# Seven products over all 16 K tiles for the second block's pairs, and a recurrence that keeps two heads' states

## The chip, the cores and the metric

One core of one Trainium2 chip runs the kernel. The metric is the time of one execution on the device, in microseconds (us), as the median of several runs; lower is better. TensorE multiplies matrices, VectorE (DVE in the profile) and ScalarE (ACT) do elementwise work, GpSimd (POOL) does a little of it and issues some transfers, SyncE (SP) issues the other transfers. PEld is TensorE's loading of weights. Rows of the profile are in us unless they say ns.

## The reference

Two transformer-like blocks follow each other on one sequence of 512 tokens of width 2048, in float32. The change touches the second block alone, and there its first projection:

```python
xn = rmsnorm_2(h, norm_gain[l])                        # 512 x 2048
proj = jnp.einsum('bsd,de->bse', xn, w_in[l])          # 2048 -> 6 * 1024
q, k, v, g_sb, x_lru, g_lru = jnp.split(proj, ...)     # 1024 columns each
...
xc = causal_depthwise_conv(x_lru, conv_w[l], conv_b[l])    # 4 taps along the tokens
r = sigmoid(xc_block @ w_a + b_a); i = sigmoid(xc_block @ w_x + b_x)   # 8 blocks of 128
a = exp(-8 * r * softplus(-lam))
u = sqrt(1 - a * a) * (i * xc)
h_t = a_t * h_(t-1) + u_t                              # along the 512 tokens
y_lru = h * silu(g_lru)
y_sb = stick_breaking_attention(q, k, v) * silu(g_sb)
out = h + concat(y_sb, y_lru) @ w_out[l]
```

x_lru is called XL in the kernel, g_lru GL and g_sb GS. Each has 1024 columns, which are eight blocks ("heads") of 128.

## The kernel before

**Products.** A float32 product is made of three matmuls: each operand is split into a high half (ScalarE casts it to float32r) and a low half (VectorE subtracts the high half from the source), and high times high, high times low and low times high are added in PSUM. `split` (L456 the cast, L457 the subtraction) does this for weights and activations. A projection has 16 K tiles of 128 rows.

**Seven products.** Columns are projected in pairs of 128-column blocks by Winograd's form of Strassen's scheme: tokens in two halves, K in two halves, the pair's two blocks as the two column halves. Seven products on sums of pieces replace eight. Each half of K has KS = 6 tiles, so 12 of the 16 K tiles go through the scheme; the last NCL = 4 are done plainly by `rest`, with two weight pieces of their own ("6" and "8"). The second block has twelve such pairs, in the order XL0, GL0, XL2, GL2, XL4, GL4, XL6, GL6, GS0, GS2, GS4, GS6 (a name with the number of its first block; texts below call the last four GS0 to GS3). `seven` emits a pair's matmuls: products 1, 4, 5, remainder, 3, remainder, 2, 7, two remainders, 9. A matmul here has 256 moving columns (half the tokens).

**Weights of a pair.** Four raw pieces (0 to 3, `load_raw`, L654, from SP) are loaded for a pair. The sums that the scheme wants are made in place, one after the other, in the raw buffers: piece 0 is read for product 1, then piece 1 is added by a transfer that adds at its destination (`sum_up`, L663, issued by GpSimd), then it is read for product 2, then VectorE adds piece 2 (L661), it is read for product 3, then a second adding transfer brings piece 3 and it is read for product 9. `produce(p, i)` splits a sum into one of four weight buffers a to d: product 1 in a, 2 in b, 4 in c, 5 in d, 3 in c once product 4 has left it, 7 in c after product 3, 9 in b after product 2. The next pair's pieces are loaded into raw buffers as they come free.

**Order.** TensorE's order is the order in which the program emits matmuls. All other engines' and queues' orders are planned over the whole program by `Plan`: each instruction gets a due time from the matmul that needs it, and at every free moment of an engine the ready instruction with the earliest due time is taken; the order found is then fixed. ScalarE, VectorE, GpSimd and SP run in that fixed order.

**Around the pairs.** `side_x2` makes the differences of the activations' quarters that the scheme needs (S1 to S4) while the v projection still runs, from copies in DRAM (x2d); the last of them is split into `big` when v is done. Results of a pair leave PSUM by `evac_a1` (L1800), `evac_b` (L1806, L1807) and `evac_a2` (L1811). XL results go into two buffers xls and to `side_lru(b)`, one call for each of the eight heads: convolution on VectorE (L1396, L1398), two products on TensorE (pss), activations on ScalarE (L1414 to L1419), the input's products on VectorE (L1420, L1421), a square root (L1429), a product on GpSimd (L1431), the scan on VectorE (L1432), the product with the gate (L1437). A head's states A, V and U take 512 columns each of the tile `ar`. There is room for four heads at a time, so the square roots, scans and gates are emitted after heads 3 and 7, for four heads. GL results are gated and stored, and fetched again by `side_lru`. Temporary tiles `e` rotate among six buffers: a new one takes the buffer of the sixth before it.

Of the kernel before, what the change touches and what calls it, by code (L numbers as in the profile page):

```python
# [16 lines left out]
P = 128  # L17
# [25 lines left out]
KS = 6  # L43
# [345 lines left out]
def hybrid_two_block_kernel(ctx: ExitStack, tc: tile.TileContext, wp, wq, wc, xT, xtok, par, lvec, cst, rg, pg, lruw, out):  # L389
# [184 lines left out]
    YO = 2 * KS * NTOK  # L574
    operands2 = Later(lambda: next_turn([("y23", [P, YO], F32R), ("ymisc", [P, KT * NTOK - YO], F32)]))
# [71 lines left out]
    def load_raw(p, r, slot):  # L647
        if p is None:
            return
        n = WS if r < 4 else NCL * P  # L650
        raw = raw_all[:, WS * slot : WS * slot + n]
        raw_slot[(p, r)] = slot
        pair_raw[(p, r)] = raw
        nc.sync.dma_start(raw, wq[p, r] if r < 4 else wc[p, r - 4])  # L654

    def sum_up(p, r, q):
# [6 lines left out]
        pool.dma_start(pair_raw[(p, r)], wq[p, q], accum_op=ALU.add)  # L663

    def produce(p, i):
# [4 lines left out]
        r = lambda k: pair_raw[(p, k)]  # L670
# [5 lines left out]
        n = NCL * P if i in (6, 8) else WS  # L676
        slot = at[place]
        w = halves(wsp_all[:, 2 * WS * slot : 2 * WS * slot + 2 * n])
# [8 lines left out]
        elif i == 4:  # L687
            load_raw(p, 4, raw_slot[(p, 1)])
        elif i == 5:
            load_raw(p, 5, raw_slot[(p, 3)])  # L690
        elif i == 6:
            w_slots[:] = [at["a"], at["d"], at["c"], at["b"]]
            load_raw(following(p), 0, raw_slot[(p, 4)])
        elif i == 8:
            load_raw(following(p), 1, raw_slot[(p, 5)])
            if p < NEW:
                sum_up(following(p), 1, 2)
        elif i == 7:
            load_raw(following(p), 2, raw_slot[(p, 2)])
            if p >= NEW:  # L700
                sum_up(following(p), 1, 2)
        elif i == 9:
            load_raw(following(p), 3, raw_slot[(p, 0)])
# [36 lines left out]
    def seven(p, ops, r, c0a, c0b, evac_a1, evac_b, evac_a2, after=None):  # L740


        HL, x23, x1s, p1s, us, wv, ts = ops
        L = 2 * HL
        X1, X2 = slice(0, HL), slice(HL, L)
        q = following(p)

        def product(i, bank, x, c, first, last, n=KS):
            w = pair_w[(p, i)]
            for j in range(n):  # L750
                for pi, (ws, xs) in enumerate(PASSES):
                    mm(r[bank][:, c], w[:, ws, j * P : (j + 1) * P], x(xs, j), first and j == 0 and pi == 0,
                       last and j == n - 1 and pi == 2)
                yield

        def rest(i, bank, c0, x1, first, last):

            w = pair_w[(p, i)]
# [10 lines left out]
        produce(p, 6)  # L769
# [3 lines left out]
        produce(p, 8)  # L773
# [1250 lines left out]
```

## Time and profile before

| | us |
|---|---|
| Median of the runs | 1689.38 (1687.52 to 1690.68) |
| The profiled execution's own time | 1691.34 |
| Its span, first to last instruction | 1689.3 |
| The twelve pairs of the second block | 1009.6 to 1279.7 of the span |

An engine's busy time is the time in which the profile shows it at work. A row of the timeline gives the start, the duration of the merged run, engine, source line, operation and tiles, the count, and in square brackets the idle time before it with what ended that. Matmuls are pipelined and the ends are modelled: the distance between starts is what they cost. The tile names of the pair stage: `wsp` weights split, `wraw` raw weights, `pj` PSUM, `y` and `x1s` the differences, `ymisc` the partial sums and the buffers xls.

### The profile page before, as it was taken

Reading aid. Unit: us, or ns where it says so; the run is one execution under the profiler, and the core shown is the slowest. Engines: PE = TensorE matmul, PEld = TensorE weight load, DVE = VectorE, ACT = ScalarE, POOL = GpSimd, SP = SyncE. Lnnn points to the kernel's source line nnn. Section 1 sums busy time; section 2 is a strip of 40 time slices with the busy share of each in tenths; the row PEclk is TensorE's granted clock in tenths of the full one; section 3 lists DMA queues with packets and bytes.
Section 4 is the critical chain, followed back from the end, with each engine's and each line's share of the span. In section 5 each row is a group of like instructions: output and inputs, shape, how many; then the busy total and the mean of one; then the engine's idle time right before and its main releaser. Section 6 shows DMA issues by size and latency. Waiting matters only on the chain.

```text
span 1689.3 us, 28307 instructions
## 1 busy us (share of the span) xinstructions
PE 1661.5 (98%) x10840; PEld 1510.2 (89%) x10840; DVE 1204.3 (71%) x2076; ACT 945.1 (56%) x1584; POOL 184.7 (11%) x205
## 2 busy tenths in 40 slices
PE   8999999999999999999999999999999999999998
PEld 8789999999999999988887779999998888888887
DVE  5784797766798989883577857998874476885433
ACT  6454566654677777673455544657643366665311
POOL 0111121111222222100000000111100000100000
PEclk9999999999999999999999999999999999999999
DMA  8435866767666566643677976666668223434233
GB/s 314 169 126 141 205 148 166 170 156 172 138 151 144 138 147 142 172 141 133 200 245 258 298 217 149 155 185 151 176 165 265 87 76 102 128 102 129 75 103 122
DMA packets 110360, 273.01 MB, mean 162 GB/s; under 512 B 11776, under 2 KB 25728, under 8 KB 108544
## 3 DMA queue, kind: packets, MB, share of 16 engines
q1 hardware_dynamic: 93712, 225.05, 41.3%
q0 software_dynamic: 16512, 46.15, 15.9%
q8 instruction: 85, 1.39, 0.3%
q14 instruction: 51, 0.42, 0.1%
HBM read 241.79 MB, written 29.36 MB: 161 GB/s over the span
## 4 chain that ended last, share of the span: by engine, by line
PE 67%; DVE 3%; DMA 2%; ACT 1%; issue 1%; SPq 0%; DVEq 0%; ACTq 0%
PE pj L489 59%; PE pmt L489 3%; PE pss L489 2%; PE ptt L492 1%; DVE wsp L457 1%; PE bank L489 1%; DMA wraw<-in_wp 1%; PE pmt L492 1%; DMA wraw<-in_wq 1%; ACT wsp L456 0%; PE pss L492 0%; DMA e<-yd 0%; DVE big L457 0%; DMA wraw<-in_wc 0%; ACT L1429 0%
## 5 line engine op out<-in xcount | busy, mean ns | idle before, releaser
L489 PE MATMUL pj<-wsp,big 128*128 128x512 f32 x3072 | 737.1, 397 | 6.5 <-DVE wsp L457 3.6
L489 PEld LDWEIGHTS pj<-wsp,big 128*128 128x128 f32 x3072 | 570.7, 188 | 138.0 <-DVE wsp L457 6.3
L457 DVE TENSOR_TENSOR wsp<-wraw,wsp 128x768 fp32r<-128x768 f32 (+3 forms) x462 | 464.8, 1012 | 232.6 <-ACT wsp L456 224.6
L456 ACT CAST wsp<-wraw 128x768 fp32r<-128x768 f32 (+3 forms) x462 | 401.2, 873 | 375.9 <-PE pj L489 283.8
L489 PE MATMUL pj<-big,wsp 128*128 128x264 f32 (+2 forms) x4224 | 541.2, 284 | 10.8 <-ACT wsp L456 7.1
L489 PEld LDWEIGHTS pj<-big,wsp 128*128 128x128 f32 x4224 | 520.6, 189 | 13.9 <-ACT wsp L456 7.5
L663 POOL DMA_DIRECT2D wraw<-in_wq x104 | 91.3, 888 | 650.4 <-DVE wsp L457 509.1
L489 PE MATMUL pj<-x,wsp 128*128 128x264 f32 x720 | 100.9, 287 | 1.9 <-DVE wsp L457 1.4
L489 PEld LDWEIGHTS pj<-x,wsp 128*128 128x128 f32 x720 | 92.5, 188 | 3.4 <-DVE wsp L457 2.3
L489 PE MATMUL pj<-x1s,wsp 128*128 128x264 f32 (+1 forms) x576 | 79.9, 289 | 3.3 <-DVE e L1800 3.3
L456 ACT CAST pt<-ptt 128x512 fp32r<-128x512 f32 (+2 forms) x96 | 50.7, 528 | 55.5 <-PE ptt L492 55.2
L457 DVE TENSOR_TENSOR pt<-ptt,pt 128x512 fp32r<-128x512 f32 (+2 forms) x96 | 59.5, 620 | 26.2 <-ACT pt L456 25.6
L489 PEld LDWEIGHTS pj<-x1s,wsp 128*128 128x128 f32 x576 | 74.6, 193 | 3.7 <-DVE e L1800 3.5
L489 PE MATMUL pss<-kk,qq 128*128 128x264 f32 x448 | 71.8, 288 | 0.0
L489 PE MATMUL pmt<-pt,vv 128*128 128x256 f32 (+1 forms) x528 | 69.3, 279 | 0.0
L489 PEld LDWEIGHTS pmt<-pt,vv 128*128 128x128 f32 x528 | 67.2, 188 | 1.6
L1271 ACT ACTIVATE e<-e,sm 128x528 f32<-128x528 f32 x64 | 47.1, 735 | 31.5 <-DVE sm L1268 31.3
L489 PEld LDWEIGHTS pss<-kk,qq 128*128 128x128 f32 x448 | 61.5, 189 | 1.3
L489 PE MATMUL pj<-y,wsp 128*128 128x256 f32 x432 | 55.6, 282 | 0.0
L489 PEld LDWEIGHTS pj<-y,wsp 128*128 128x128 f32 x432 | 53.4, 189 | 0.0
L492 PE MATMUL ptt<-ident,e 128*128 128x128 f32 x336 | 52.5, 273 | 0.0
L1268 DVE CUSTOM_DVE_ANT_0 e<-pss,ar 128x528 f32<-128x528 f32 x64 | 44.9, 702 | 7.8 <-PE pss L489 7.5
(285 smaller groups left out, 1542.0 us busy)
## 6 DMA issues: line engine op xcount, KB each, us to landing
wraw<-in_wp SPq DMA_DIRECT2D x166, 512.0 KB, 4.1
wraw<-in_wq SPq DMA_DIRECT2D x128, 384.0 KB, 3.9
wraw<-in_wq POOLq DMA_DIRECT2D x104, 384.0 KB, 5.1
wraw<-in_wc SPq DMA_DIRECT2D x64, 256.0 KB, 2.9
gated<-e SPq DMA_DIRECT2D x40, 256.0 KB, 3.1
e<-in_xT SPq DMA_DIRECT2D x28, 264.0 KB, 4.9
early<-in_xtok SPq DMA_DIRECT2D x4, 1024.0 KB, 7.4
e<-yd SPq DMA_DIRECT2D x16, 256.0 KB, 4.2
```

Of the source, the lines that this page charges most:

```text
L456: act.copy(hi, src)
L457: dve.tensor_tensor(lo, src, f(hi), ALU.subtract)
L489: _queue(nc.tensor.matmul(out, lhsT, rhs, start=start, stop=stop).ins, cost)
L492: _queue(nc.tensor.transpose(out, in_, identity).ins, 110.0)
L663: pool.dma_start(pair_raw[(p, r)], wq[p, q], accum_op=ALU.add)
L1268: dve.tensor_tensor_reduce(out=halves(x), in0=s[:, :, :HL], in1=halves(bias[:, b0 : b0 + L]), scale=1.0, scalar=3e38, op0=ALU.add, op1=ALU ...
L1271: act.activation(x, x, AF.Exp, scale=-1.0, bias=nm, accum_out=l[:, m : m + 1])
```

## The change

Pairs of the second block take KS2 = 8 tiles in each half of K, so that all 16 K tiles go through the seven products. Remainders, their pieces and their buffers are gone there. Raw pieces and weight buffers of these pairs are 1024 columns wide (before 768, and 512 for the remainders); the fourth raw buffer lies in `ar`, the fourth weight buffer takes the place of the tile `kk`. The operands of the scheme grow to eight tiles each: y23 fills its tile, x1s gets a second part in the tile `pt`, and partial sums and xls move into `ar`. The next pair's first two pieces are loaded after `produce` 4 and 5. Half of the second output block is written at once from product 2's sum (`take_t`), which saves one addition. A, V and U have room for two heads, so square roots, scans and gates are emitted after each second head. The first block's pairs are as before.

```diff
-KS = 6
+KS, KS2 = 6, 8
...
-    operands2 = Later(lambda: next_turn([("y23", [P, YO], F32R), ("ymisc", [P, KT * NTOK - YO], F32)]))
+    operands2 = Later(lambda: next_turn([("y23", [P, 2 * KS2 * NTOK], F32R)])[0])
...
     def load_raw(p, r, slot):
...
+        if p >= NEW:
+            raw = raw_all[:, 1024 * slot : 1024 * slot + 1024] if slot < 3 else ar[:, 3072:4096]
+            nc.sync.dma_start(raw, wq2[p - NEW, r])
+        else:
+            raw = raw_all[:, WS * slot : WS * slot + (WS if r < 4 else NCL * P)]
+            nc.sync.dma_start(raw, wq[p, r] if r < 4 else wc[p, r - 4])
...
     def sum_up(p, r, q):
...
-        pool.dma_start(pair_raw[(p, r)], wq[p, q], accum_op=ALU.add)
+        pool.dma_start(pair_raw[(p, r)], wq2[p - NEW, q] if p >= NEW else wq[p, q], accum_op=ALU.add)
...
     def produce(p, i):
...
-        n = NCL * P if i in (6, 8) else WS
+        n = KS2 * P if p >= NEW else NCL * P if i in (6, 8) else WS
...
+        if p < NEW:
+            w = halves(wsp_all[:, 2 * WS * slot : 2 * WS * slot + 2 * n])
+        else:
+            w = halves(wsp_all[:, 2048 * slot : 2048 * slot + 2048]) if slot < 3 else wsp3[:]
...
         elif i == 4:
-            load_raw(p, 4, raw_slot[(p, 1)])
+            if p < NEW:
+                load_raw(p, 4, raw_slot[(p, 1)])
+            else:
+                load_raw(q, 0, raw_slot[(p, 1)])
         elif i == 5:
-            load_raw(p, 5, raw_slot[(p, 3)])
+            if p < NEW:
+                load_raw(p, 5, raw_slot[(p, 3)])
+            else:
+                w_slots[:] = [at["a"], at["d"], at["c"], at["b"]]
+                load_raw(q, 1, raw_slot[(p, 3)])
...
-    def seven(p, ops, r, c0a, c0b, evac_a1, evac_b, evac_a2, after=None):
+    def seven(p, ops, r, c0a, c0b, evac_a1, evac_b, evac_a2, after=None, take_t=None):
...
+        whole = 2 * KS == KT
...
         def rest(i, bank, c0, x1, first, last):
+            if whole:
+                return
...
-        produce(p, 6)
+        if not whole:
+            produce(p, 6)
...
-        dve.tensor_tensor(ts[:], r[0][:, :HL], us[:], ALU.add)
+        if whole:
+            yield from take_t(r[0][:, :HL], us[:])
+        else:
+            dve.tensor_tensor(ts[:], r[0][:, :HL], us[:], ALU.add)
...
+    x1sb = [Later(lambda: T([P, 2, KS, H2], "x1s", F32R)), Later(lambda: T([P, 2, KS2 - KS, H2], "pt", F32R))]
+    wsp3 = Later(lambda: T([P, 2, 1024], "kk", F32R))
+    misc2 = [ar[:, 4096 + i * H2 : 4096 + (i + 1) * H2] for i in range(4)]
+    xls = [ar[:, 5120 + i * NTOK : 5120 + (i + 1) * NTOK] for i in range(2)]
...
     def side_x2():
...
-        for j in range(KS):
+        for j in range(KS2):
...
-        split(big[:, 0, :KS, H2:NTOK], big[:, 1, :KS, H2:NTOK], s4)
+        split(big[:, 0, :KS2, H2:NTOK], big[:, 1, :KS2, H2:NTOK], s4)
...
-                n = min(8, 2 * KS - 8 * k8)
-                pool.dma_start(x2d[k8, t][:, : n * P], flat(xg[:, :n]))
+                pool.dma_start(x2d[k8, t], flat(xg))
...
     def A(b):
-        return ar[:, (b % 4) * 512 : (b % 4 + 1) * 512]
+        return ar[:, (b % 2) * 512 : (b % 2 + 1) * 512]
...
     def side_lru(b):
...
-                   *([("ydone", b - 4)] if b > 3 else []))
+                   *([("ydone", b - 2)] if b > 1 else []))
...
-        if b % 4 == 3:
+        if b % 2:
...
-                for i in range(b - 3, b + 1):
+                for i in range(b - 1, b + 1):
...
-            for i in range(b - 3, b + 1):
+            for i in range(b - 1, b + 1):
                 yield when(("gl", i))
                 y = et(NTOK)
...
-                    w_slots[:] = [3, 2, 0, 1]
+                    w_slots[:] = [2, 1, 3, 0]
...
-                for k in range(0, KS, 2):
+                for k in range(0, KS2, 2):
```

## Rows read from the trace of the kernel before

**Rows 1.** The page's first part: the span, then busy time, share of the span and instructions of TensorE and VectorE.

```profile
span 1689.3 us, 28307 instructions
...
PE 1661.5 (98%) x10840; PEld 1510.2 (89%) x10840; DVE 1204.3 (71%) x2076; ACT 945.1 (56%) x1584; POOL 184.7 (11%) x205
```

**Rows 2.** The page's chain that ended last, shares of the span by line.

```profile
PE pj L489 59%; PE pmt L489 3%; PE pss L489 2%; PE ptt L492 1%; DVE wsp L457 1%; PE bank L489 1%; DMA wraw<-in_wp 1%; PE pmt L492 1%; DMA wraw<-in_wq 1%; ACT wsp L456 0%; PE pss L492 0%; DMA e<-yd 0%; DVE big L457 0%; DMA wraw<-in_wc 0%; ACT L1429 0%
```

**Rows 3.** Busy time by stretch (start:end, length, busy time and instructions of each engine, mean granted clock of TensorE, busy share of the transfer engines, GB/s): XL and GL pairs, GS0, the last three pairs; and, from a second such table, two pairs in the middle.

```profile
1009.60:1189.60 180.00, 175.78 (x1437) 172.96 (x1436) 155.62 (x241) 108.76 (x155) 24.08 (x24) 1.00 0.64 162
1189.60:1217.90 28.30, 24.98 (x183) 24.51 (x182) 23.51 (x37) 20.62 (x28) 4.61 (x4) 0.88 0.69 189
1217.90:1279.70 61.80, 61.80 (x525) 61.70 (x523) 44.48 (x70) 26.91 (x39) 4.34 (x5) 1.00 0.64 173
...
1062.08:1106.06 43.98, 43.98 (x362) 43.43 (x360) 40.40 (x64) 30.28 (x43) 6.60 (x7) 1.00 0.60 154
```

**Rows 4.** Timeline of TensorE, from 1017 to 1250.

```profile
1017.40 0.50 PE L489 MATMUL pj<-big,wsp 128*128 128x256 f32 x2 [1.15 <-ACT wsp L456]
...
1119.78 4.25 PE L489 MATMUL pj<-big,wsp 128*128 128x256 f32 x34 [0.89 <-DVE wsp L457]
...
1128.04 3.55 PE L489 MATMUL pj<-big,wsp 128*128 128x256 f32 x28 [1.62 <-DVE wsp L457]
...
1151.65 1.56 PE L489 MATMUL pss<-qq,vv 128*128 128x512 f32 x6
1153.05 1.93 PE L489 MATMUL pj<-big,wsp 128*128 128x256 f32 x15
...
1177.56 1.57 PE L489 MATMUL pj<-big,wsp 128*128 128x256 f32 x12
...
1205.83 4.21 PE L489 MATMUL pj<-x1s,wsp 128*128 128x256 f32 x18 [3.32 <-DVE e L1800]
...
1229.22 2.32 PE L489 MATMUL pj<-x1s,wsp 128*128 128x256 f32 x18
...
1248.40 1.57 PE L489 MATMUL pj<-big,wsp 128*128 128x256 f32 x12
1249.81 2.32 PE L489 MATMUL pj<-x1s,wsp 128*128 128x256 f32 x18
```

**Rows 5.** VectorE's groups by line and form, 960 to 1005, while v is projected: line, engine, operation, tiles, shapes, count, busy us, mean ns of one, idle before.

```profile
L457 DVE TENSOR_TENSOR wsp<-wraw,wsp 128x1024 fp32r<-128x1024 f32 x16 | 19.4, 1220 | 12.5 <-ACT wsp L456 12.5
```

**Rows 6.** The same view of VectorE, 1062.08 to 1106.06.

```profile
L457 DVE TENSOR_TENSOR wsp<-wraw,wsp 128x768 fp32r<-128x768 f32 x14 | 13.3, 949 | 1.9 <-ACT wsp L456 1.8
L661 DVE TENSOR_TENSOR wraw<-wraw 128x768 f32<-128x768 f32 x4 | 3.8, 951 | 0.2 <-DMA wraw<-in_wq 0.2
L457 DVE TENSOR_TENSOR wsp<-wraw,wsp 128x512 fp32r<-128x512 f32 x4 | 3.6, 890 | 0.5 <-ACT wsp L456 0.5
```

**Rows 7.** The same view of ScalarE, 960 to 1005.

```profile
L456 ACT CAST wsp<-wraw 128x1024 fp32r<-128x1024 f32 x15 | 15.7, 1048 | 11.4 <-DMA wraw<-in_wp 7.4 <-PE pj L489 3.8
```

**Rows 8.** Timeline of ScalarE: in GS0, and the cast of product 7's weights in the third GS pair.

```profile
1198.45 1.28 ACT L1429 ACT_TABLE_LOAD   x1
...
1200.40 1.28 ACT L1417 ACT_TABLE_LOAD   x1
...
1202.41 0.80 ACT L1418 ACTIVATE ar<-e,lrup 128x512 f32<-128x512 f32 x1
...
1203.64 1.55 ACT L456 CAST wsp<-wraw 128x768 fp32r<-128x768 f32 x2
...
1248.48 0.84 ACT L456 CAST wsp<-wraw 128x768 fp32r<-128x768 f32 x1 [3.59 <-PE pj L489]
```

**Rows 9.** Timeline of VectorE: the split into big before the pairs; the low half of product 7's weights in GL6; GS0; the low halves for product 3 and 7 in the third GS pair.

```profile
997.48 1.76 DVE L457 TENSOR_TENSOR big<-ar,big 128x1536 fp32r<-128x1536 f32 x1 [0.44 <-ACT big L456]
...
1179.61 0.96 DVE L457 TENSOR_TENSOR wsp<-wraw,wsp 128x768 fp32r<-128x768 f32 x1
...
1203.77 0.69 DVE L1421 SCALAR_TENSOR_TENSOR ar<-e,ar 128x512 f32<-128x512 f32 x1 [0.44 <-ACT e L1419]
...
1205.36 0.42 DVE L1800 TENSOR_TENSOR e<-pj,ymisc 128x256 f32<-128x256 f32 x1
...
1243.75 0.96 DVE L457 TENSOR_TENSOR wsp<-wraw,wsp 128x768 fp32r<-128x768 f32 x1 [0.21 <-ACT wsp L456]
...
1249.40 0.95 DVE L457 TENSOR_TENSOR wsp<-wraw,wsp 128x768 fp32r<-128x768 f32 x1
```

**Rows 10.** The adding transfers of line L663, 1018 to 1280 (23 of them): time from GpSimd's issue to landing.

```profile
DMA to landing us min/median/max: 4.7/5.3/7.0
```

**Rows 11.** The transfers of 1217.9 to 1259 (41.1 us): the queue of GpSimd's transfers with packets, MB and share of the 16 engines' time, and SP's loads of raw pieces with count, size and median time to landing.

```profile
q0 software_dynamic: 576, 1.57, 25.6%
...
wraw<-in_wq SPq DMA_DIRECT2D x8, 384.0 KB, 4.1
```

**Rows 12.** Timeline of GpSimd: the adding transfer after the split for product 3 in the third GS pair.

```profile
1245.11 0.87 POOL L663 DMA_DIRECT2D wraw<-in_wq  x1 [12.69 <-DVE wsp L457]
```

**Rows 13.** Line L1429 (the square roots) over the whole span: count, duration in ns (least, median, most), first and last start.

```profile
L1429 ACT ACT_TABLE_LOAD  x8: 1283/1283/1283, 1061.4 to 1205.8; - x8
L1429 ACT ACTIVATE ar<-ar x8: 631/632/634, 1062.7 to 1207.1; 128x512 f32<-128x512 f32 x8
```

More of the change, by code (lines that the diff above doesn't have):

```diff
@@ L388, in hybrid_two_block_kernel @@
 @with_exitstack
-def hybrid_two_block_kernel(ctx: ExitStack, tc: tile.TileContext, wp, wq, wc, xT, xtok, par, lvec, cst, rg, pg, lruw, out):
+def hybrid_two_block_kernel(ctx: ExitStack, tc: tile.TileContext, wp, wq, wq2, wc, xT, xtok, par, lvec, cst, rg, pg, lruw, out):
     nc = tc.nc
@@ L738, in fm_all, with product @@
         return fm(unit, [(ps[0][:, :HL], (0, HL)), (ps[1][:, :HL], (HL, L))], after_kt)
-    def seven(p, ops, r, c0a, c0b, evac_a1, evac_b, evac_a2, after=None):
-        HL, x23, x1s, p1s, us, wv, ts = ops
+    def seven(p, ops, r, c0a, c0b, evac_a1, evac_b, evac_a2, after=None, take_t=None):
+        HL, KS, x23, x1, p1s, us, wv, ts = ops
         L = 2 * HL
+        whole = 2 * KS == KT
         X1, X2 = slice(0, HL), slice(HL, L)
         q = following(p)
-        def product(i, bank, x, c, first, last, n=KS):
+        def product(i, bank, x, c, first, last):
             w = pair_w[(p, i)]
-            for j in range(n):
+            for j in range(KS):
                 for pi, (ws, xs) in enumerate(PASSES):
-                    mm(r[bank][:, c], w[:, ws, j * P : (j + 1) * P], x(xs, j), first and j == 0 and pi == 0,
-                       last and j == n - 1 and pi == 2)
+                    mm(r[bank][:, c], w[:, ws, j * P : (j + 1) * P], x(xs, j), (first or whole) and j == 0 and pi == 0,
+                       (last or whole) and j == KS - 1 and pi == 2)
                 yield
         def rest(i, bank, c0, x1, first, last):
+            if whole:
+                return
             w = pair_w[(p, i)]
@@ L988, in side_x2 @@
         a, b = fetch(0)
-        for j in range(KS):
-            later = fetch(j + 1) if j + 1 < KS else None
+        for j in range(KS2):
+            later = fetch(j + 1) if j + 1 < KS2 else None
             dve.tensor_tensor(b[:, H2:], a[:, H2:], b[:, H2:], ALU.subtract)
@@ L1825, in pair2 @@
             yield from seven(pair_no[((name, i), (name, i + 1))], ops2, banks2, 0, 0, evac_a1, evac_b, evac_a2,
-                             after if last else None)
+                             after if last else None, take_t)
         for k, (name, i) in enumerate(SECOND):
```

70 lines of the change are left out of this document (35 added, 35 removed).

## The prediction

> **What bounds the kernel now.** I read the page first: TensorE is busy for 98% of the span and VectorE for 71% [rows 1], and the chain that ended last runs through TensorE, 59% of the span in the projection matmuls alone [rows 2]. An average hides the stage of the change, so the table by stretch comes next, cut at the pairs' borders [rows 3]. The twelve pairs take 1009.6 to 1279.7, 270.1 us: eight pairs of XL and GL with seven heads of the recurrence (180.0), GS0 with the eighth head (28.3), three GS pairs (61.8). Last I read TensorE's timeline [rows 4]: two undisturbed GS pairs start the same product 20.59 us apart (1229.22 and 1249.81), for 174 matmuls, so 0.1183 us each; a head's six wide matmuls take 1.40 (1151.65 to 1153.05).
>
> A floor follows for each stretch. XL and GL: 8 x 20.59 + 7 x 1.40 = 174.5, so 5.5 of 180.0 is lost, and the timeline shows most of it: 1.2 before the first pair's leftover weights, 0.9 and 1.6 around 1119 and 1128, where VectorE's split came late. GS0: 20.59 + 1.40 = 22.0, so 6.3 of 28.3 is lost: a wait of 3.3 for L1800, and a granted clock of 0.88 on average [rows 3], which is full speed but for some 6.8 us at half. The last three pairs: 61.8, nothing lost. So TensorE bounds the stage, but only just: in the undisturbed two pairs from 1062 to 1106 VectorE is busy for 40.4 of 43.98 us, 92% [rows 3].
>
> **Matmuls removed.** Before: 7 x 6 x 3 = 126, and four remainder groups of 4 x 3, 174 a pair. After: 7 x 8 x 3 = 168. Twelve pairs save 72 x 0.1183 = **8.5 us**, on the bounding engine.
>
> **VectorE and ScalarE.** Seven splits of 1024 columns replace seven of 768 and two of 512. A VectorE half of 1024 takes 1.22 us [rows 5], of 768 0.95, a sum of 768 0.95 [rows 6]; a ScalarE cast of 1024 1.05 [rows 7], of 768 0.84 [rows 8]. For two pairs VectorE gains 14 x 0.27 + 4 x 0.27 for the sums, and loses four splits of 512 (0.68 when nothing else touches them; the mean of 0.89 includes shared stretches) and two adds of 0.42 [rows 9]: 3.8 + 1.1 - 2.7 - 0.8 = +1.4. TensorE's two pairs shrink to 43.98 - 12 x 0.1183 = 42.56; VectorE then wants 41.8 of it, 98%. That is the price of the change: not work, but room. In the GS pairs VectorE is busy for 44.5 of 61.8 [rows 3] and has room.
>
> **The refills get a shorter cover.** Products 3 and 7 use the weight buffer of the product before the last. Before, 30 matmuls lay between, 3.55 us; now 24, 2.84. The high half must stand at the first matmul, the low half at the third, 0.24 later: 3.08. In a GS pair product 3 ends as the next run starts at 1248.40, the cast starts at 1248.48 and the low half is done at 1249.40 + 0.95: 1.95 after [rows 4, 8, 9]. In GL6 it was 1180.57 - 1177.56 = 3.0, because the recurrence stood in front [rows 4, 9]. The longer instructions add 0.21 + 0.27. GS: 2.4 against 3.08, hidden, with 0.65 to spare. XL and GL: between 2.4 and 3.5, so 0 to 0.4 late, and more where VectorE is fuller. Two refills in nine pairs: 0 to 7.6 us if each is 0.4 late; I take **4**, the middle.
>
> The Trainium skill (Perfetto Trace Analysis, Optimizing Scalar/DVE Operations) speaks against this edit: where these engines are not saturated but make bubbles elsewhere, smaller instructions may finish sooner. No row here shows smaller ones; by that rule the time would be that of the third rival.
>
> **The accumulating transfer.** Product 9's weights need raw piece 0 plus piece 3, and that sum is a transfer that GpSimd issues after the split for product 3 has read piece 0. Before, 120 matmuls (14.2 us) lay between the end of product 4 and product 9; now 96, 11.36, and 11.6 with the low half's 0.24. At 384 KB the transfer lands 4.7 to 7.0 us after issue, median 5.3 [rows 10]. Four of them took 25.6% of the 16 engines in 41.1 us, 2.63 us each [rows 11]; a third more bytes is 0.9, so 6.2. Chain in a GS pair: 2.4 (the refill), 0.4 from the low half's end (1243.75 + 0.96) to GpSimd's issue (1245.11) [rows 9, 12], 6.2, then 1.05 + 1.22 + 0.1: 11.4 against 11.6, just hidden. In XL and GL the refills are up to 1.1 later and the last split some 0.4: 12.9, so 1.3 late, of which the stalls at 3 and 7 have already paid 0.5. 8 pairs x 0.8 = 6; the lower end is 0, the upper, at a landing of 7.9, 1.7 more in all twelve. I take **4**: TensorE's stalls also let VectorE catch up.
>
> The skill (DMA: Bandwidth & Descriptors, Anatomy of one DMA) fits 2.0 us plus bytes over 436 GB/s for a transfer of this queue, so 0.3 us for the added 128 KB. The trace is far slower, 2.63 us of moving for 384 KB; these transfers also add. By the page the chain above would be 0.6 shorter and the 4 us about 1.
>
> The load of piece 2 (4.1 us on SP [rows 11], some 4.9 with 512 KB), added to piece 1 on VectorE before product 4's split, has the same 11.6 us: 3.5 + 4.9 + 1.4 + 2.5 = 12.3 at worst. I take **1** (0 to 4). Together the new stalls are 9.
>
> **Two heads at a time.** The code before groups four square roots, but its trace shows eight table loads for eight square roots [rows 13]: they already run singly. So the smaller groups add no load; cost 0. What moves is the end of each head: the gate's four e tiles (y) after head 7 come as two. In GS0 product 2 waits for L1800, which frees the bank. It ran at 1205.36, behind L1421 at 1203.77, which in turn waited on ScalarE for two table loads (1198.45, 1200.40); the cast of product 7's weights, too, ran only at 1203.64 [rows 8, 9]. L1800 writes a new e tile and inherits the sixth before it: th, a2, four y, then this, so head 7's th, which L1418 read until 1203.2 [rows 8]. With two y it inherits one that GL6 freed. I take **-5** (0 to -6.3). The stalls around XL4, when four gates arrive together, should halve: **-1.5** (0 to -2.5). The first pair's wait for leftover weights goes, but its chain through piece 0 is as tight as any: **-0.5** (0 to -1.2).
>
> **Costed at nothing.** Two more rounds of differences before the pairs: about 2 x 3 us of VectorE, which waits for most of the time from 984 to 1009; the last piece, the split into big, ran at 997.48 [rows 9] and grows by a third. If that cover went, 3 us. The wider copies of x2 and the fourth fetch at the end lie beside matmuls that don't use them. Two loads a pair leave SP's queue; the others grow.
>
> **Sum.** -8.5 - 5 - 1.5 - 0.5 + 4 + 4 + 1 = **-6.5 us**. The profiled execution took 1691.3, 2.0 above the median of 1689.4; a change within 0.2% (3.4 us) can't be told from none. From the median: **1683 us**.
>
> **Rivals.**
> 1. All new chains are hidden: planned by due time, refills go first and the recurrence waits for the GS pairs' room. The GS pairs' handoffs of 1.95 speak for it, the 98% against. -8.5 - 6.3 - 3.7, with 1 of stalls: 1672.
> 2. VectorE becomes the bound. If it can't pass the 92% that it reached without a stall, two pairs take 41.8 / 0.92 = 45.4, not 43.98: four times +1.4 is +5.7. With -5 in GS0 and 18 x 0.1183 = -2.1 in the last three: 1688, no change.
> 3. The accumulating transfer ends each pair late. Against savings of 8.5 + 7 it decides from 1.3 us a pair. With landings of 7.9 instead of 6.2 the chain is 1.7 longer: about 2.5 late in eight XL and GL pairs, 0.7 in four others, 23 us: 1689.4 - 15.5 + 23 = 1697, slower. For it: landings up to 7.0 now. Against: two loads a pair that shared the wires with it are gone.
>
> **How the numbers follow.** The forecast (1677 to 1686) has 0.45, rival 1 0.17, rival 2 0.20, rival 3 0.18. Faster is the forecast and rival 1: 0.62; same 0.20; slower 0.18. The range of 1672 to 1696 leaves out half of rivals 1 and 3. The likeliest case's own range is 1677 to 1686.
>
> **What would show it.** 168 matmuls a pair at 0.118; GS pairs of 19.9 us without a wait; no 3.3 us wait for the evacuation in GS0 and no half clock there; eight table loads at the square roots again; in XL and GL pairs short waits of TensorE for the weights' cast or low half, mostly before products 3, 7 and 9, some 9 us in all; VectorE at 95% or more. The forecast is wrong if those waits pass 15 us, if they also stand in the GS pairs (then the transfer is the cause), or if a long one brings the half clock back.

## The result: slower, not faster

The changed kernel takes 1697.4 us (median of 6 runs, 1696.1 to 1697.9) beside 1689.2 of the kernel before on the same chip: ratio 1.0045, 95% interval 1.0034 to 1.0055, so 8 us slower. I had forecast 1683, within 1672 to 1696, and faster. The profiled execution took 1696.1. Its page and its table by stretch, with the columns of [rows 3]: all twelve pairs, then XL and GL, GS0, and the last three pairs.

```profile
span 1694.0 us, 28007 instructions
PE 1657.8 (98%) x10768; PEld 1504.2 (89%) x10768; DVE 1219.0 (72%) x2053; ACT 950.6 (56%) x1565; POOL 182.6 (11%) x205
...
1006.00:1285.90 279.90, 261.22 (x2066) 254.98 (x2065) 232.65 (x309) 156.88 (x193) 32.66 (x34) 0.98 0.65 173
...
1006.00:1195.40 189.40, 177.14 (x1388) 172.37 (x1387) 162.80 (x219) 110.31 (x137) 23.99 (x25) 0.97 0.65 170
1195.40:1224.30 28.90, 23.23 (x176) 22.56 (x175) 22.54 (x29) 20.26 (x26) 4.32 (x4) 0.94 0.52 146
1224.30:1285.90 61.60, 60.85 (x507) 60.05 (x506) 47.31 (x63) 26.31 (x31) 4.35 (x5) 1.00 0.71 195
```

72 matmuls are gone (10840 to 10768). The stage should then be 2016 x 0.1183 + 8 x 1.4 = 249.7 us; it is 279.9, so 30.2 are lost, where before 11.9 of 270.1 were. XL and GL lose 189.4 - 168.8 = 20.6 (5.5 before), GS0 28.9 - 21.3 = 7.6 (6.3 before), the last three pairs 61.6 - 59.6 = 2.0 (0 before). TensorE's waits from 1000 to 1300, grouped by what ended them (us in total, times, longest), first before (1.0 of its 4.1 us lies behind the stage), then after:

```profile
PE pj L489 <- DVE wsp L457: 4.1, 4, 1.6
PE pj L489 <- DVE e L1800: 3.3, 1, 3.3
PE pj L489 <- ACT wsp L456: 1.2, 1, 1.2
```

```profile
PE pj L489 <- DVE kk L457: 5.8, 8, 1.6
PE pj L489 <- DVE e L1824: 4.8, 1, 4.8
PE pj L489 <- ACT kk L456: 3.8, 2, 3.1
PE pj L489 <- DVE wsp L457: 3.6, 4, 2.1
PE pj L489 <- ACT wsp L456: 0.5, 1, 0.5
```

The wait for the evacuation in GS0 (L1824, L1800 before) is still there and longer. New are 9.6 us for the fourth weight buffer, kk: 4.0 of them before product 3 of the first pair, 5.7 before product 4 of seven pairs. These are idle times. From start to start, against 0.1183 us a matmul, each wait costs about 0.16 more, 21.1 us in all instead of 18.5. A single product's wait is counted so below, unless its row is shown. Four stretches of 3.4 us at half clock cost 1.7 each, 6.8 together; before, there was one of 6.8 us, which cost 3.4. Waits and half clock add up to 27.9 of the 30.2; the other 2.3 are not assigned.

Two places tell the story. **The first pair** takes 30.8 us from its first matmul to the next pair's, where its matmuls need 19.9; before, it took 22.9 where they needed 20.6. So 10.9 us are lost instead of 2.3. Rows of SP, GpSimd, ScalarE, VectorE and TensorE (L652 loads raw pieces, L665 is the adding transfer, L663 VectorE's sum, once L661):

```profile
1000.51 1.46 SPq L652 DMA_DIRECT2D wraw<-in_wq  x2
...
1007.09 0.91 POOL L665 DMA_DIRECT2D wraw<-in_wq  x1 [0.25 <-issue]
...
1013.99 1.05 ACT L456 CAST wsp<-wraw 128x1024 fp32r<-128x1024 f32 x1 [3.99 <-DMA wraw<-in_wq]
...
1016.54 1.22 DVE L663 TENSOR_TENSOR wraw<-wraw 128x1024 f32<-128x1024 f32 x1
...
1018.97 0.50 PE L489 MATMUL pj<-y,kk 128*128 128x256 f32 x2 [3.08 <-ACT kk L456]
1020.36 1.86 PE L489 MATMUL pj<-y,kk 128*128 128x256 f32 x7 [0.89 <-DVE kk L457]
```

Piece 0 is loaded only at 1000.51, because its raw buffer still held the last unit of v. From there one thing hangs on another: split for product 1, adding transfer (issued 1007.09, the cast that it frees starts 1013.99, 6.9 later), split for product 2, VectorE's sum of piece 2, split for product 3. Product 3 finds its weights 4 us late. Product 9 comes 2.3 us late as well, for another reason. Rows of ScalarE, VectorE and TensorE:

```profile
1027.70 1.06 ACT L456 CAST wsp<-wraw 128x1024 fp32r<-128x1024 f32 x1 [1.28 <-DMA wraw<-in_wq]
1030.26 0.42 DVE L1833 TENSOR_TENSOR ar<-pj,ar 128x256 f32<-128x256 f32 x1 [0.95 <-PE pj L489]
...
1031.33 1.22 DVE L457 TENSOR_TENSOR wsp<-wraw,wsp 128x1024 fp32r<-128x1024 f32 x1
1032.60 7.25 PE L489 MATMUL pj<-big,wsp 128*128 128x256 f32 x46 [2.14 <-DVE wsp L457]
```

The adding transfer of piece 3 was issued 1.1 us behind the next pair's first one, and landed at 1027.6. Its cast was done at 1028.8. But in VectorE's fixed order the low half stands behind the evacuation of product 7 (L1833), which waits until TensorE has finished product 7, and so it is done only at 1032.55. A stretch at half clock follows each of the two waits.

**The third and fourth pairs**, around 1070. First GpSimd's rows of before, at the hand-over from the second pair to the third, the closest of that stage; then the rows of after, with SP, VectorE and TensorE:

```profile
1040.43 0.85 POOL L663 DMA_DIRECT2D wraw<-in_wq  x1 [12.14 <-DVE wsp L457]
1047.17 0.84 POOL L663 DMA_DIRECT2D wraw<-in_wq  x1 [5.88 <-DVE wsp L457]
```

```profile
1068.81 0.89 POOL L665 DMA_DIRECT2D ar<-in_wq  x1 [1.50 <-DVE kk L457]
1069.95 0.87 POOL L665 DMA_DIRECT2D wraw<-in_wq  x1 [0.24 <-DVE ar L1824]
...
1074.09 0.33 SPq L652 DMA_DIRECT2D wraw<-in_wq  x1
...
1081.36 1.22 DVE L457 TENSOR_TENSOR wsp<-wraw,wsp 128x1024 fp32r<-128x1024 f32 x1
1082.50 0.42 DVE L1838 TENSOR_TENSOR ar<-pj,ar 128x256 f32<-128x256 f32 x1
1082.83 2.35 DVE L663 TENSOR_TENSOR wraw<-wraw 128x1024 f32<-128x1024 f32 x2
...
1077.59 0.50 PE L489 MATMUL pj<-big,wsp 128*128 128x256 f32 x2 [0.54 <-ACT wsp L456]
1078.85 5.69 PE L489 MATMUL pj<-big,wsp 128*128 128x256 f32 x46 [0.76 <-DVE wsp L457]
1085.26 0.50 PE L489 MATMUL pj<-y,kk 128*128 128x256 f32 x2 [0.72 <-ACT kk L456]
1086.97 3.37 PE L489 MATMUL pj<-y,kk 128*128 128x256 f32 x18 [1.21 <-DVE kk L457]
```

Before, a pair's last adding transfer and the next pair's first were issued 6.7 us apart there; in the stage the 24 issues lie 6.7 to 17.5 us apart, and none was made while another was under way. After, these two lie 1.1 us apart, and the two of nine of the eleven hand-overs 1.1 to 2.3. The transfers of 1068 to 1081 (KB each, median us to landing):

```profile
ar<-in_wq POOLq DMA_DIRECT2D x1, 512.0 KB, 7.6
wraw<-in_wq POOLq DMA_DIRECT2D x1, 512.0 KB, 10.0
wraw<-in_wq SPq DMA_DIRECT2D x1, 512.0 KB, 6.4
```

The first of the two is late for product 9 (TensorE at 1077.59 and 1078.85). The second delays product 2's split to 1081.36. Piece 2, loaded at 1074.09 into the same traffic, landed at 1080.5; its sum stands behind that split in VectorE's fixed order and starts at 1082.83. So product 4's weights come 2 us late (1085.26, 1086.97). All 24 adding transfers of after against [rows 10]:

```profile
DMA to landing us min/median/max: 5.4/6.5/10.0
```

Why the issues moved together I read from the code, and no run tests it alone: the buffer of product 1 was used again by a remainder product, so the next pair's first split had to wait; without remainders it is free early, and that split, with its transfer, comes right behind product 3's.

### The profile page after: what moved, and what is told of

Read it like the earlier page. It is cut to its first block, busy times and chain, and to the rows that moved or that the text cites. A ratio compares the mean times of both kernels' runs of the same rounds, so it can differ in the third digit from the quotient of the medians.

```text
span 1694.0 us, 28007 instructions
## 1 busy us (share of the span) xinstructions
PE 1657.8 (98%) x10768; PEld 1504.2 (89%) x10768; DVE 1219.0 (72%) x2053; ACT 950.6 (56%) x1565; POOL 182.6 (11%) x205
## 3 DMA queue, kind: packets, MB, share of 16 engines
q1 hardware_dynamic: 92912, 226.36, 41.1%
## 4 chain that ended last, share of the span: by engine, by line
PE 59%; DVE 6%; issue 4%; ACT 2%; DMA 2%; POOL 0%; DVEq 0%; POOLq 0%; ACTq 0%
PE pj L489 52%; PE pmt L489 3%; PE pss L489 2%; DVE wsp L457 2%; PE ptt L492 1%; DMA wraw<-in_wq 1%; PE bank L489 1%; DVE kk L457 1%; DMA wraw<-in_wp 1%; ACT wsp L456 1%; PE pmt L492 1%; DVE wraw L663 1%; ACT kk L456 0%; PE pss L492 0%; DMA ar<-in_wq 0%
## 5 line engine op out<-in xcount | busy, mean ns | idle before, releaser
L457 DVE TENSOR_TENSOR wsp<-wraw,wsp 128x1024 fp32r<-128x1024 f32 (+3 forms) x386 | 407.4, 1059 | 213.0 <-ACT wsp L456 205.9
L456 ACT CAST wsp<-wraw 128x1024 fp32r<-128x1024 f32 (+3 forms) x386 | 350.6, 912 | 310.5 <-PE pj L489 247.5
L489 PE MATMUL pj<-big,wsp 128*128 128x264 f32 (+2 forms) x3648 | 471.9, 284 | 11.0 <-ACT wsp L456 6.9
L489 PEld LDWEIGHTS pj<-big,wsp 128*128 128x128 f32 x3648 | 451.8, 190 | 14.4 <-ACT wsp L456 7.3
L665 POOL DMA_DIRECT2D wraw<-in_wq x96 | 84.1, 888 | 532.2 <-DVE wsp L457 297.7
L489 PE MATMUL pj<-y,kk 128*128 128x256 f32 x576 | 77.4, 290 | 9.7 <-DVE kk L457 5.8
L489 PEld LDWEIGHTS pj<-y,kk 128*128 128x128 f32 x576 | 73.0, 195 | 11.9 <-DVE kk L457 7.7
L457 DVE TENSOR_TENSOR pt<-ptt,pt 128x512 fp32r<-128x512 f32 (+2 forms) x96 | 59.6, 620 | 26.2 <-ACT pt L456 25.6
L456 ACT CAST kk<-wraw 128x1024 fp32r<-128x1024 f32 x28 | 29.3, 1047 | 48.7 <-PE pj L489 34.8
```

Source lines behind the costliest of these rows:

```text
L456: act.copy(hi, src)
L457: dve.tensor_tensor(lo, src, f(hi), ALU.subtract)
L489: _queue(nc.tensor.matmul(out, lhsT, rhs, start=start, stop=stop).ins, cost)
L665: pool.dma_start(pair_raw[(p, r)], wq2[p - NEW, q] if p >= NEW else wq[p, q], accum_op=ALU.add)
```

## The experiments

In every ratio the reference is the kernel before on the same chip. That kernel took 1687.7 to 1689.2 us on the chips used, so what one changed kernel gains on another is worked out from their ratios. Each edit also lets the planner find another order; in e11, where nothing else changes, the ratio is 0.0028 above the changed kernel's, 5 us. A single difference of that size says little. "Stage" is the twelve pairs of the profiled run, from the first matmul's start to the last one's end: 270.1 before, 279.9 after.

**e1**, the kernel before with the recurrence two heads at a time: `b % 4` becomes `b % 2` in A, V, U and in the grouping.

> The kernel before with one part of the change: the recurrence keeps two heads. The prediction gave this part -5 in the GS0 pair and -1.5 around XL4: 1683. The theory after seeing the changed trace: the GS0 wait for L1800 stays, because the evacuation's e tile is opened after the two y tiles, and these wait for stores and for head 7; only the 2.5 us around XL4 and GL4 go: 1686 to 1688, with a wait of 3 us or more in GS0. Rival: fewer e tiles are enough and the wait goes: 1681 to 1684.

1689.3 us beside 1687.7, ratio 1.0010 (0.9999 to 1.0021). The wait in GS0 shrank (1.7 for 3.5) and the wait around 1119 went, but XL6 and GL6 got waits of 2.9 in place of these. This half of the change gains nothing by itself.

**e11**, the changed kernel in another order: `HOP = 40.0` to `HOP = 55.0`.

> The changed kernel with the planner's cost of a hand-over between engines at 55 instead of 40: it computes the same, with the instructions of the side work in another order. If the 8 us between the two kernels are the chain of the weights (raw buffer, load, adding transfers, sum, split), this order has them too: 1692 to 1703 us. Rival (the 8 us are the luck of one order, which any reshuffling throws away): below 1689 us.

1700.8, ratio 1.0073 (1.0046 to 1.0100). Stage 279.2, with the longest waits in the same places (4.1 before product 3 of the first pair, 5.4 in GS0). So the loss isn't the luck of this one order.

**e6**, VectorE relieved: three of the four taps of the recurrence's convolution are left out.

> The changed kernel without the three later taps of the convolution (its result is then another): 24 instructions of 0.74 us, 2 a pair in the XL and GL pairs, 16 us of VectorE's time in all. VectorE-full theory: the waits before product 4 in GL2, GL6 and GS0 (5.0 us) and those before product 9 in XL2 (1.6) go, 6 to 8 us less, about 1690. Rival, chains of transfers and of the fixed order: the waits in XL0 (5.1 and 2.3) and in GS0 (4.9) stay, and those before product 4 in the GS pairs, where VectorE has room, too: 1694 to 1697.

1698.5, ratio 1.0058 (1.0043 to 1.0073). The stage row and the waits:

```profile
1007.30:1289.20 281.90, 262.98 (x2066) 256.76 (x2065) 219.33 (x285) 156.92 (x193) 32.55 (x34) 0.97 0.64 172
```

```profile
PE pj L489 <- DVE kk L457: 6.1, 8, 1.4
PE pj L489 <- ACT kk L456: 5.0, 4, 3.0
PE pj L489 <- DVE e L1821: 3.9, 1, 3.9
PE pj L489 <- DVE wsp L457: 3.8, 4, 2.1
```

VectorE is busy 13 us less, and nothing is gained: the long waits are those of the changed kernel, and the short ones moved among the pairs (product 4 of GL6 from 1.7 to 0.6, of XL6 from none to 2.4, of GS4 from 0.5 to 2.2). These 13 us of VectorE's work are not what slows it.

**e2**, the first half of GS0's output into xls[0], so that it opens no new e tile; **e3**, the first pair's pieces in raw buffers that come free earlier; **e5**, both.

```diff
-                out[0] = xls[0] if name == "XL" else et(NTOK)
+                out[0] = xls[0] if name == "XL" or (name, i) == ("GS", 0) else et(NTOK)
-                        load_raw(NEW, r, r)
+                        load_raw(NEW, r, (2, 1, 0, 3)[r])
```

> The changed kernel, where the first half of GS0's result goes into the free buffer xls[0] instead of a new e tile. E-tile theory: the wait of 4.8 us before product 2 of GS0 goes, and with it the half clock behind it: 6 us less than the changed kernel, about 1691. Rival, VectorE and ScalarE are full there and the order of the recurrence is the cause: the wait moves to product 7 or 9 and the time stays at 1697, within 2.

> The changed kernel, where the first pair's raw piece 0 goes into the raw buffer that comes free first (2) and piece 2 into the one that comes free late (0). Theory: piece 0 lands near 1000 instead of 1004, the chain split 1, adding transfer, split 2, sum, split 3 ends some 4 us earlier, and the waits of 4 us before product 3 of XL0 go, with the half clock behind them: 1692 to 1694. Rival: the chain is bound by the later pieces or by VectorE, and piece 2 now comes late: 1697, within 2.

> The changed kernel with both edits: piece 0 of the first pair in raw buffer 2, and GS0's first half in xls[0]. Theory of separate places: the 4.9 us before product 2 of GS0 and the half clock behind it go as well: 6 us less than with the first edit alone, 1681 to 1682. Rival, the GS0 wait only moves to the next refills, as it did without the first edit (-1.7 in the median): 1686 to 1688.

e2: 1695.7, ratio 1.0047 (1.0031 to 1.0064). The wait of 4.8 before product 2 is gone, but product 1 of the next pair waits 2.0 instead, for VectorE's L1830, and product 4 of GS4 2.5. e3: 1687.6, ratio 0.9994 (0.9984 to 1.0003), some 9 us better than after. The first pair takes 24.4 us instead of 30.8. But its product 3 starts no earlier than in the changed kernel (1018.97):

```profile
1019.45 0.50 PE L489 MATMUL pj<-y,kk 128*128 128x256 f32 x2 [0.91 <-ACT kk L456]
```

Its wait is shorter because product 1 starts 3.1 us later; the adding transfer ahead of product 2 lands at 1014.6, in the changed kernel at 1013.9. So the theory, an earlier chain through piece 0, isn't what happened. What changed lies behind it. The first pair's last adding transfer is issued ahead of the next pair's first one, the two of a hand-over lie 1.5 to 4.7 us apart instead of mostly 1.1 to 2.3 and land in 5.9 (median) instead of 6.5, and the waits before product 9 of XL0 and XL2 are gone. Those before product 4 are not: 1.6 in each of GL2, GL4 and GL6, 2.2 in GS4. e5: 1685.0, ratio 0.9982 (0.9973 to 0.9992), between its two forecasts.

**e7**, the kernel before with pieces 0 and 3 exchanged in the first pair's raw buffers (`(3, 1, 2, 0)[r]`); **e12**, that and e2's edit.

> The kernel before with the same edit of the first pair: piece 0 in the raw buffer that comes free first (3), piece 3 in 0. Theory, the chain through piece 0 binds the first pair only since the change: before, the first pair waits for the leftover's weights (1.3 and 0.7) and nothing moves: 1688, within 2. Rival, any reshuffling of the raw buffers gives the planner a better order: 3 us less or more.

> The kernel before with the two edits that it can take: the first pair's piece 0 in raw buffer 3 (e7) and the fixed buffer for the first half of the recurrence's first gated pair. If the wait of 3 us in that pair goes without another in its place, 1681 to 1683 us; if the next product waits instead, as in e2, 1684 to 1685 us. Against e10 it says how much of the gain belongs to the new split of the work and how much to edits that both kernels take.

e7: 1684.6, ratio 0.9977 (0.9967 to 0.9986). e12: 1681.9, ratio 0.9963 (0.9953 to 0.9973). e7's theory, that nothing moves, falls: both edits pay in the kernel before as well. With like edits the change costs less: e3 against e7 0.17% (0.9994, 0.9977) and e5 against e12 0.19% (0.9982, 0.9963), some 3 us, instead of 0.45%. So of the 9 us that e3 gains, about 4 are gained without the change too. The stage of e12 is 264.3 us, 6 above its 258.2 of matmuls.

**e8**, the changed kernel without the first adding transfer: `if p >= NEW and q == 1: return`.

> The changed kernel without the first adding transfer of the second block's pairs (product 2 then has piece 0 alone, another result): the disputed cost by itself. Collision theory: the one left lands in 5.4 to 5.7 us instead of 5.4 to 7.6, the load of piece 2 in 4 instead of up to 6.4, the first pair's chain loses 7 us; the waits before product 3 of XL0, before product 9 and before product 4 of GL2 go: 10 us less, about 1687, with GS0's wait left. Rival, VectorE and the recurrence set the waits: only XL0's goes: 1692.

1680.5, ratio 0.9951 (0.9936 to 0.9966): 16 us less than after, and below both forecasts. The stage is 263.5 us, the transfers that are left land in 5.6 (median, most 6.7), and the waits are:

```profile
PE pj L489 <- DVE e L1826: 4.6, 1, 4.6
PE pj L489 <- DVE wsp L457: 2.1, 3, 1.5
PE pj L489 <- DVE kk L457: 1.6, 4, 0.8
```

The 9.6 us for kk are 1.6, though the load of piece 2 and the sum behind it are still made. So the waits for kk came from the transfer, and product 4's not from its own chain alone. The first pair takes 21.1 us here, 9.7 less than after, which is more than half of the stage's gain of 16.4. No run leaves the transfer out of the kernel before, but there the whole stage has only 11.9 us to give.

**e16**, without VectorE's sum of pieces 1 and 2 (product 4's weights from piece 1 alone); **e13**, without both of VectorE's sums with piece 2, into piece 1 and into piece 0 (its expectation and e14's speak of the first only); **e14**, as e13 and without the first adding transfer; **e17**, as e16 and without that transfer.

```diff
 e16    if p >= NEW and (r, q) == (1, 2): return
 e13    if p >= NEW and q == 2: return
 e14    if p >= NEW and q < 3: return
 e17    if p >= NEW and (r, q) in ((1, 2), (0, 1)): return
```

> The changed kernel without VectorE's sum of pieces 1 and 2 alone in the second block: product 4's weights come from piece 1 only (another result); VectorE's sum of piece 2 into piece 0 stays, which e13 had taken away as well. Theory (product 4's chain of load, sum and split is what costs): the waits before product 4 go as in e13, 1686 to 1690 us. Rival (what helped in e13 was the other sum, between products 2 and 3, which releases raw buffers and hands the second adding transfer its start): 1692 us or more.

> The changed kernel without VectorE's sum of pieces 1 and 2 in the second block: the weights of product 4 are made from piece 1 alone (another result), so that they wait for neither piece 2 nor the sum; both adding transfers stay. Theory (the chain of product 4 costs some 7 us by itself, and its waits bring stretches at half clock): the waits of the fourth weight buffer before product 4 go, those before product 9 and in the gated pair stay: 1686 to 1691 us. Rival (the adding transfers are the root, and TensorE only meets product 4 first): the time moves to the products behind it, 1694 us or more.

> The changed kernel with neither VectorE's sum of pieces 1 and 2 nor the first adding transfer in the second block (another result); the adding transfer of piece 3 stays. Theory: what e8 still waited for before product 4 goes too, and the one wait of 4.8 us in the first gated pair of the recurrence and the 249.7 us of matmuls stay: stage 255 to 259 us, 1671 to 1677 us. Rival (without the transfer the chain of product 4 is hidden anyway): as e8, 1679 to 1682 us.

> As e16 and also without the first adding transfer (another result); against e14 it keeps VectorE's sum of piece 2 into piece 0. Theory (the chain of product 4 and the transfers share the loss): 1673 to 1677 us, stage 255 to 259 us. Rival (the sum between products 2 and 3 is late too): 1679 us or more, with waits before products 3 and 9.

e16: 1695.0, ratio 1.0040 (1.0028 to 1.0052), stage 278.4. My theory that product 4's chain costs 7 us by itself falls: without its sum the ratio differs from after's by 0.0005, which is less than the width of either interval, and products 3, 7 and 9 wait in its place. e13: 1686.4, ratio 0.9986 (0.9975 to 0.9997). e14: 1673.5, ratio 0.9907 (0.9886 to 0.9928). e17: 1672.8, ratio 0.9906 (0.9886 to 0.9927); its stage and all of its waits:

```profile
1009.00:1263.00 254.00, 252.32 (x2066) 248.56 (x2065) 219.26 (x297) 157.20 (x193) 22.82 (x22) 1.00 0.60 166
```

```profile
PE pj L489 <- DVE wsp L457: 1.8, 4, 0.8
```

The matmuls' saving is real: 254.0 of a possible 249.7 us, no half clock, and GS0 waits for nothing long. What a sum costs depends on the transfer. With both transfers in place the sum of 1 and 2 is worth nothing that can be told from noise (after to e16); with the first transfer gone it is worth 7.6 (e8 to e17). The sum into piece 0 is worth 9 with both transfers (e16 to e13) and nothing without (e17 to e14). So each of the two steps that piece 0's buffer loses pays: the transfer, and, where the transfer stays, the sum. I take this to say that piece 0's row of steps is too long: four splits, one sum and two transfers in one buffer, one after the other. That transfers meet is not enough for the loss: in e13 they land in 5.4 to 9.7 us, median 6.5, as late as in the changed kernel, and it is 10 us faster. How the 16 us of e8 divide between a shorter row and transfers that no longer meet isn't told apart.

**e4**, the sum of pieces 0 and 1 by GpSimd in place of the first adding transfer (here piece 1 has piece 2 in it by then, so the weights of product 2 hold another sum); **e9**, by VectorE, ahead of the sum of 1 and 2; **e10**, e9 with e2's and e3's edits; **e18**, as e10 but that sum by GpSimd; **e15**, as e18 with the sum of piece 2 into piece 0 on GpSimd as well.

```diff
 e9, e10
-        if p >= NEW and q == 2:
-            dve.tensor_tensor(pair_raw[(p, r)], pair_raw[(p, r)], pair_raw[(p, 2)], ALU.add)
+        if p >= NEW and q < 3:
+            dve.tensor_tensor(pair_raw[(p, r)], pair_raw[(p, r)], pair_raw[(p, q)], ALU.add)
 e18    (pool if q == 1 else dve).tensor_tensor(...)
 e15    (pool if r == 0 else dve).tensor_tensor(...)
```

> The changed kernel, where the sum of pieces 0 and 1 is made by GpSimd from the loaded piece 1, so that one adding transfer is left for a pair instead of two. Theory, the two transfers issued within 1.1 to 2.4 us slow each other (5.4 to 10.0 us to landing, median 6.5): the remaining one lands within 5.5 to 6, the waits before product 9 (2.3 and 1.6 us) and most of those before product 4 (7 us in all) go: 6 to 9 us less, 1688 to 1691. Rival, VectorE is full (98% in XL and GL pairs): GpSimd's add takes its turn from VectorE, and the waits before product 4 stay: 1697 or more.

> The changed kernel with one edit: in the second block the sum of pieces 0 and 1 is made by VectorE from the piece 1 that is already loaded, not by an adding transfer; the sum of pieces 1 and 2 is put behind it. One adding transfer a pair is left and VectorE gets 8 more sums of 1,024 columns, 8 x 1.22 = 9.8 us. Theory (the adding transfers, issued close together, end the chains of the weights late): as in e8, which only left that transfer out, the stage loses its waits before product 9 and most of those before product 4: 1680 to 1685 us. Rival (VectorE is the bound, or its fixed order hands each added sum on to TensorE as a wait): at least 1697, up to 1707.

> The changed kernel with three edits together: VectorE's sum of pieces 0 and 1 in place of the adding transfer (e9), the first pair's pieces in raw buffers 2, 1, 0, 3 (e3), and the fixed buffer for the first half of the recurrence's first gated pair (e2). Theory: the gains of e8 (17 us) and of the wait in that gated pair (some 4 us less the wait that follows it) nearly add up, and the buffers of e3 bring little beside e8, whose first pair waits for nothing: 1672 to 1680 us, faster than both kernels. Rival (the same slack is gained three times): no better than e8, 1680 us or more.

> As e10, but the sum of pieces 0 and 1 alone goes to GpSimd (2.6 us by e4's rows); e15 had moved VectorE's sum of piece 2 into piece 0 there as well, which stands in the short way from product 2 to product 3. Theory (VectorE's three sums a pair are what e10 lost against e8): 1676 to 1682 us. Rival (piece 1 has to be read by GpSimd before VectorE adds piece 2 to it, which puts 2.6 us into product 4's chain): 1686 us or more.

> As e10 (first pair's raw buffers 2, 1, 0, 3; fixed buffer in the first gated pair; no first adding transfer), but the sum of pieces 0 and 1 is made by GpSimd, 2.6 us each by e4's rows, and emitted ahead of the sum of pieces 1 and 2. Theory (what e10 lost against e8 is VectorE's 1.22 us in the chain before product 4): 1675 to 1680 us, the fastest kernel with the same result. Rival (piece 1 must be read by GpSimd before VectorE may add piece 2 to it, and GpSimd's sum takes longer than VectorE's): 1684 to 1692 us, no better than e10.

e4: 1704.5, ratio 1.0095 (1.0077 to 1.0113). e9: 1689.4, ratio 1.0006 (0.9995 to 1.0017). e10: 1683.8, ratio 0.9976 (0.9966 to 0.9987). e18: 1696.6, ratio 1.0051 (1.0033 to 1.0069). e15: 1714.6, ratio 1.0151 (1.0129 to 1.0172). e10 and e18 came out as their rivals say, e9 between its two forecasts, e15 worse than both of its own. A GpSimd sum took 2.6 us or more (e18's group: 2619, 2623 and 2932 ns) beside 1.22 on VectorE, and in all but e4 piece 1 must be read before piece 2 may be added to it. In e18 no two adding transfers meet (landings 5.7), yet TensorE waits 9.9 us for kk behind VectorE. With 2.4 more for its cast, 8.0 of these stand before product 7, which reads `big`, and 3.5 before product 4:

```profile
1144.95 2.17 PE L489 MATMUL pj<-big,kk 128*128 128x256 f32 x16 [1.92 <-DVE kk L457]
```

So the lateness is not in product 4's chain alone, and no run shows by which way it reaches product 7. e9 makes 12 more sums on VectorE, not the 8 that its expectation says, and keeps 7 of e8's 16 us. Whether the other 9 are the sums' place in the chain or VectorE's time isn't told apart: in e10's stage VectorE is busy 245.2 of 265.8 us, 92%.

e10 beats the kernels before and after, but e12, which leaves the change out, is as fast or faster (0.9963 and 0.9976, with overlapping intervals).

## Why the prediction was wrong

The step that failed is the price of the weights' chains: each was held against its own cover in a steady pair, product 4 at +1, and the first pair at -0.5. Measured, product 4 comes 6.9 us late (0.5 of it in the first pair), and the first pair alone loses 8.6 us more than before, half clock included. GS0, taken at -5, lost 1.3 us more than before, and the half clock was left out of the sum. Leaving out one of the chain's transfers gives 16 us back (e8), and with one sum also left out 23 (e17, whose stage is 4 us above its matmuls). The prediction's own signs of being wrong came: waits of more than 15 us (18.5) and a long one that brings the half clock back.

- **Matmuls removed, -8.5: right.** e17's stage lies 16 us below that of before, and its 1672.8 us is what rival 1 gave for all chains hidden. But it leaves two sums out; with them the chains are not hidden.
- **GS0, -5: wrong.** It lost 7.6 instead of 6.3. I had put the wait down to the e tile that L1800 inherits, and took it to go with that tile. VectorE's rows show what stands in front of it now:

```profile
1212.45 0.69 DVE L1445 SCALAR_TENSOR_TENSOR ar<-e,ar 128x512 f32<-128x512 f32 x1
1213.05 0.69 DVE L1444 SCALAR_TENSOR_TENSOR ar<-ar,e 128x512 f32<-128x512 f32 x1
1213.65 0.42 DVE L1824 TENSOR_TENSOR e<-pj,ar 128x256 f32<-128x256 f32 x1
...
1214.12 3.91 PE L489 MATMUL pj<-x1s,wsp 128*128 128x256 f32 x18 [4.77 <-DVE e L1824]
```

  L1824 follows at once on head 7's arithmetic, and TensorE on L1824. The e tile is one link: in e2, with a buffer of its own, the wait went. But then product 1 of the next pair waited 2.0, and the kernel gained nothing that can be told from noise; in e17, with other work around L1824 in VectorE's order, the wait was gone with the e tile still there. I had priced a wait by its last link.
- **First pair, -0.5: wrong sign.** Its waits before products 1, 4 and 3 rose from 2 to 5 us; product 9's 2.3 come on top, and two half-clock stretches cost 3.4. The text called the chain through piece 0 "as tight as any" and did not add it up. Summed from the rows it was there to see: a load, a transfer of six to seven, three splits and a sum, against three products of 2.84. Which transfer goes first at the hand-over, and VectorE's order before product 9, were not.
- **Refills of 3 and 7, +4: too high.** Outside the first pair they wait for nothing that counts; product 5 of XL6 waits 0.5.
- **Product 9, +4: right in size (2.3 + 1.6 = 3.9) by luck, wrong in kind.** I had looked for 0.8 in each of eight pairs, with every landing at 6.2. It is two waits, in XL0 and XL2. In XL0 the low half stood in VectorE's order behind an evacuation; in XL2 the landing was late. Transfers alone land in 5.6 (e8, e17), quicker than 6.2; two together in up to 10.0. I took the landing as a property of the size, not of what else is issued.
- **Product 4, +1: far too low.** 6.9 us, among them 2.3 in GL2 and 1.7 in GL6. I had added the chain up without VectorE's fixed order. In GL2 the sum stands there behind a split that itself waits for an adding transfer; in GL6 VectorE works without a gap from 1166 to 1178, and the low half stands behind two other sums.
- **XL4 and GL4, -1.5: about right.** The waits around 1119 and 1128 of before (2.5) have no successor but 0.4. In e1, which has only this part of the change, 1.2 of them stayed and XL6 and GL6 waited 2.9, so the cause that I gave is not shown.
- **Half clock: not in the sum.** It was only named as a way to be wrong. 6.8 us instead of 3.4.

Rival 2 (VectorE the bound) is not what e6 shows: with 13 us less of its work the time stayed. VectorE does come near the forecast's 98% where TensorE runs on: in XL4 and GL4 it is busy for 40.7 of 43.4 us, 94%. Rival 3 had the cause, the accumulating transfer, and its time, 1697, but not the way: it counted on landings of 7.9 and stalls of 2.5 in every pair, and the runs show pairs of transfers that meet, a first pair with 8.6 us of the loss, and a third of the waits at product 4. That its time fits is luck.

The Trainium skill (DMA: Bandwidth & Descriptors, Anatomy of one DMA) gives 2.0 us plus bytes over 436 GB/s for a transfer of GpSimd's queue, 3.2 us by estimate for 512 KB. The runs do not agree, for transfers that add at their destination: 5.2 at the least (e8), 5.6 in the median alone, 10.0 beside another.

## What to carry over

Add up the whole row of steps that one buffer goes through in a period, transfers included, and hold it against the period, before pricing each step against its own cover; here one buffer goes through four splits, a sum and two transfers, and leaving out one of these gave 9 to 16 us. Add up the first period apart, where the buffers come free late: here it held 8.6 us of the loss. And give the kernel before the same small edits that help the changed one, before the two are compared: here that took the change's cost from 0.45% to 0.19%. When a change removes work between two transfers, ask how far apart they will be issued, not only how large they are. Here 8.5 us saved on the bounding engine, 3% of the stage, were lost because it then waited longer for its weights.

## What the runs showed of the hardware

I had not expected adding transfers to be so much slower together: 512 KB landed in 5.2 to 7.7 us with one a pair (e8, e17), and in 6.4 to 10.0 where it was issued 1.1 to 2.3 us behind another (nine transfers of the changed kernel). The plain load beside the two of 1069 and 1070 took 6.4, the eight loads ahead of it 3.4 to 4.9. Nor had I expected the half clock behind waits of a few us. The rows (columns as in [rows 3]; the third number from the end is the granted clock) are the wait before product 3 of the first pair, the stretch behind it, the next, and that behind GS0's wait:

```profile
1016.40:1019.80 3.40, 0.50 (x2) 0.30 (x2) 3.21 (x4) 2.05 (x2) 0.20 (x1) 1.00 0.01 2
1019.80:1023.20 3.40, 2.84 (x13) 2.84 (x14) 0.51 (x1) 0.00 (x0) 1.57 (x2) 0.50 0.57 78
1023.20:1026.60 3.40, 3.40 (x30) 3.40 (x30) 1.94 (x3) 2.00 (x2) 0.00 (x0) 1.00 1.07 207
...
1214.30:1217.70 3.40, 3.40 (x17) 3.40 (x18) 1.22 (x1) 1.34 (x2) 1.29 (x1) 0.50 0.65 254
```

After waits of 3.1 and 0.9 us, and of 4.8, TensorE ran at 1.2 GHz: 17 matmuls in 3.4 us, behind GS0's wait, where 30 ran at 2.4 GHz. The other two stretches followed the wait of 2.1 us before 1032.6 (half from 1033.4) and those of 1.3 and 1.9 us at 1077 and 1086 (half from 1088.0). No stretch followed the wait before 1177.0, where TensorE was idle for 1.55 us, and in e17, where no wait was longer than 0.8, the clock stayed at 1.00.
